# Nearest upsampling by two: the first store copied by VectorE alone and issued by ScalarE

## The chip, the core and the metric

The kernel runs on one core of a Trainium2 chip. The metric is device time in microseconds: the median of 3 runs is 196.97 us (196.87 to 197.55). Of the core's engines the kernel uses VectorE (DVE in the profile) and ScalarE (ACT) to copy, and SyncE (SP) and ScalarE to issue transfers between the chip's main memory (DRAM) and its on-chip memory, which has 128 partitions. The transfers of both issuers run on the core's 16 DMA engines. What SyncE issues stands in one queue (q1 in the profile), what ScalarE issues in another (q10). GpSimd (POOL) and TensorE (PE) do nothing in the kernel but take part in its start and its close.

## The reference

The input is float32 of shape 16 x 64 x 64 x 64 (16.78 MB), the output 16 x 64 x 128 x 128 (67.11 MB). Every input element is written to a block of two by two output elements:

```
for i in range(new_h):
    for j in range(new_w):
        src_i = i // scale_factor
        src_j = j // scale_factor
        result[:, :, i, j] = x[:, :, src_i, src_j].copy()
```

Nothing is computed. One input row of 64 elements becomes two equal output rows of 128, that is 256 elements.

## The kernel before

The 65536 input rows (batch, channel and height taken together) are spread over the 128 partitions, 512 rows each, and every partition's rows are contiguous in main memory, in the input and in the output. So each partition's work is: bring in 512 rows of 64 elements, expand each to 256 elements, write them out.

One tile `mem` holds everything (lines 186 to 188). Its back part `xt` is the input, 512 x 64 elements; its front part of `WF` = 20224 elements is free at first. The expanded rows of a step go to a piece of `mem`, called `u`, and are stored from there.

Three loads are issued by SyncE at the very start (lines 192 to 195, moved ahead of the start barrier by `begin_before_barrier`): rows 0 to 31, rows 32 to 287, rows 288 to 511, being 1, 8 and 7 MB (in the profile's KB: 1024, 8192, 7168). All stand in SyncE's queue, in this order.

Then nine steps, called tiles 0 to 8 here, with 54, 38, 54, 61, 54, 63, 63, 63 and 62 rows (line 181). Each step makes two copies and one store (lines 212 to 216). VectorE expands the first `kv` rows (line 213), ScalarE the others (line 214), both through an access pattern that reads each element twice along the row and each row twice. In tiles 1 to 8 `kv` is five eighths of the rows, cut to an even number: 22, 32, 38, 32, 38, 38, 38, 38. In tile 0 it is all rows but one: 53 on VectorE, 1 on ScalarE. Tile 0 needs the first two loads, since its rows go up to 53.

Store n is issued once both copies of tile n are done. Stores 3 and 5 are issued by ScalarE, the other seven by SyncE. An issuing engine works off its instructions in the order in which the program lists them, and waits at each for what it needs; on ScalarE that means the order copy 0, copy 1, copy 2, copy 3, store 3, copy 4 and so on.

Where the pieces lie sets the order around the change (lines 206 to 208). Tiles 0, 2, 4, 6, 8 lie at the front of `mem`, from element 0 on, so tile 2 may be written only when store 0 has landed, tile 4 when store 2 has landed, and so on. Tiles 1, 3, 5, 7 end where the input rows of their step begin, so they write over input rows that earlier steps have expanded: tile 1's copies wait for VectorE's copy of tile 0, and tile 3's wait for store 1. There are thus two buffers in turn, and a store's landing is what lets the step after next begin. The tile framework puts in these waits by itself.

`close_early` arranges the end of the program: the final wait is on the last SyncE store, the others are waited for by GpSimd earlier.

Of the kernel before, what the change touches and what calls it, by code (L numbers as in the profile page):

```python
# [153 lines left out]
@with_exitstack  # L154
def kernel(
    ctx: ExitStack,
    tc: tile.TileContext,
    x: bass.AP,
    scale_factor: int,
    out: bass.AP,  # L160
):
    nc = tc.nc
    nc.at_finalize(begin_before_barrier)
    nc.at_finalize(close_early)
    P = nc.NUM_PARTITIONS
    s = int(scale_factor)
    B, C, H, W = x.shape
    R = B * C * H // P
    fdt = x.dtype

    xp = x.rearrange("b c h w -> (b c h) w").rearrange("(p r) w -> p r w", p=P)
    op = out.rearrange("b c (h hd) w -> (b c h) (hd w)", hd=s).rearrange(
        "(p r) w -> p r w", p=P
    )

    rows = [54, 38, 54, 61, 54, 63, 63, 63, 62]
    GROW = s * s
    FREE = 79
    WF = FREE * GROW * W
    assert sum(rows) == R
    mem_pool = ctx.enter_context(tc.tile_pool(name="mem", bufs=1))
    mem = mem_pool.tile([P, WF + R * W], fdt, name="mem")
    xt = mem[:, WF:].rearrange("p (r w) -> p r w", r=R)

    HEAD = 32
    cuts = [0, HEAD, R // 2 + HEAD, R]
    for lo, hi in zip(cuts, cuts[1:]):
        nc.sync.dma_start(out=xt[:, lo:hi], in_=xp[:, lo:hi])  # L195

    def expanded(r0, r1):
        return (
            xt[:, r0:r1].unsqueeze(2).unsqueeze(4).to_broadcast([P, r1 - r0, s, W, s])
        )  # L200

    r0 = 0
    before = (0, 0)
    for n, k in enumerate(rows):
        size = k * GROW * W
        at = 0 if n % 2 == 0 else WF + r0 * W - size
        assert at >= before[1] or at + size <= before[0]
        before = (at, at + size)
        u = mem[:, at : at + size].rearrange(
            "p (k a w b) -> p k a w b", k=k, a=s, w=W  # L210
        )
        kv = k - 1 if n == 0 else k * 5 // 8 & ~1
        nc.vector.tensor_copy(out=u[:, :kv], in_=expanded(r0, r0 + kv))  # L213
        nc.scalar.copy(out=u[:, kv:], in_=expanded(r0 + kv, r0 + k))  # L214
        issuer = nc.scalar if n in (3, 5) else nc.sync
        issuer.dma_start(out=op[:, r0 : r0 + k, :], in_=u)  # L216
        r0 += k

# [34 lines left out]
```

## Time and profile before

| quantity | value |
|---|---|
| median of 3 runs | 196.97 us (196.87 to 197.55) |
| profiled execution, own time | 197.08 us |
| its span | 195.7 us |
| VectorE busy | 52.3 us in 9 instructions |
| ScalarE busy | 42.1 us in 10 instructions |
| moved by DMA | 83.89 MB, mean 429 GB/s |
| VectorE, 53 rows of tile 0 (L213) | 14.29 us |
| ScalarE, 1 row of tile 0 (L214) | 0.40 us |
| issue of store 0 by SyncE | at 38.48 us, landed 57.44 |
| issue of store 1 by SyncE | at 42.11 us, landed 68.95 |

The times in the profile count from the span's start. "SPq" and "ACTq" are the issuing sequencers of SyncE and ScalarE. In a group of instructions the columns are the line, the engine, the operation, output and input tile, the shapes (partitions x elements), the count, then the busy time in us and the mean in ns of one, then the idle time of the engine just before them and what ended it. The chain that ended last has the start, the duration and the work of each piece. A DMA's duration in the chain runs from its issue to its landing, so it holds the time in which it stood in its queue behind others. Beside these views the trace records each packet of each DMA (queue, start, duration, size); a packet here is one partition's share of a transfer.

### The profile page before, as it was taken

The page shows a single profiled execution, that of the slowest core. Times are in us where ns is not written, and L with a number is a line of the kernel's source. Part 1 is how long each engine was busy: PE and PEld are TensorE (multiplying, and loading weights), DVE is VectorE, ACT ScalarE, POOL GpSimd, SP SyncE. Part 2 cuts the span into 40 slices and gives each one's busy share as a digit, 9 for nine tenths or more (in the row PEclk, how much of TensorE's full clock was granted, in tenths as well). Part 3 has the DMA queues.
Part 4 walks back from the last instruction along what each step waited for, and adds up shares of the span by engine and source line. Part 5 has one row for each costly group of instructions (what it writes and reads, how often), then busy time and mean ns, then how long its engine had stood idle before and what let it go on. Part 6 is the DMA issues. An engine that isn't in the chain of part 4 may idle for free.

```text
span 195.7 us, 102 instructions
## 1 busy us (share of the span) xinstructions
DVE 52.3 (27%) x9; ACT 42.1 (21%) x10; POOL 0.2 (0%) x4
## 2 busy tenths in 40 slices
DVE  0000099940026081000627200055540063000000
ACT  2000000150029700000694000059700073000000
POOL 0000000000000000000000000000000000000000
DMA  9999989889898989989999899999999999999994
GB/s 429 429 429 429 402 375 562 375 362 542 362 435 382 540 384 441 490 385 406 408 476 475 362 482 488 416 422 422 422 422 422 422 422 422 435 499 493 428 441 208
DMA packets 1728, 83.89 MB, mean 429 GB/s; under 512 B 192, under 2 KB 192, under 8 KB 192
## 3 DMA queue, kind: packets, MB, share of 16 engines
q1 hardware_dynamic: 1440, 67.63, 80.1%
q10 hardware_dynamic: 288, 16.25, 19.2%
HBM read 16.78 MB, written 67.11 MB: 429 GB/s over the span
## 4 chain that ended last, share of the span: by engine, by line
DMA 65%; ACT 11%; DVE 7%; SPq 0%; issue 0%; DVEq 0%; ACTq 0%
DMA out_dram<-mem 53%; DMA mem<-in_x_dram 12%; ACT mem L214 11%; DVE mem L213 7%; SPq L195 0%; DVEq L213 0%; ACTq L214 0%; SPq L216 0%
## 5 line engine op out<-in xcount | busy, mean ns | idle before, releaser
L213 DVE COPY mem<-mem 128x9728 f32<-128x9728 f32 (+3 forms) x9 | 52.3, 5818 | 111.0 <-DMA out_dram<-mem 86.9
L214 ACT COPY mem<-mem 128x6400 f32<-128x6400 f32 (+5 forms) x9 | 40.8, 4530 | 119.6 <-DMA out_dram<-mem 84.4
L214 ACT ACT_TABLE_LOAD x1 | 1.3, 1283 | 1.7 <-PEq L234 1.7
L234 POOL MEMSET const-bfloat16-1.0<- 128x1 bf16 x1 | 0.1, 101 | 0.0
L234 POOL MEMSET const-uint8-127<- 128x1 uint8 x1 | 0.1, 101 | 0.0
L234 POOL MEMSET const-float32-0.0<- 128x1 f32 x1 | 0.1, 98 | 0.2 <-issue 0.2
L234 POOL MEMSET const-float32-1.0<- 128x1 f32 x1 | 0.1, 98 | 0.0
## 6 DMA issues: line engine op xcount, KB each, us to landing
out_dram<-mem SPq DMA_DIRECT2D x3, 6912.0 KB, 30.1
out_dram<-mem SPq DMA_DIRECT2D x2, 8064.0 KB, 27.8
out_dram<-mem ACTq DMA_DIRECT2D x1, 8064.0 KB, 29.9
out_dram<-mem SPq DMA_DIRECT2D x1, 7936.0 KB, 32.3
out_dram<-mem ACTq DMA_DIRECT2D x1, 7808.0 KB, 29.3
mem<-in_x_dram SPq DMA_DIRECT2D x1, 7168.0 KB, 40.2
out_dram<-mem SPq DMA_DIRECT2D x1, 4864.0 KB, 26.8
mem<-in_x_dram SPq DMA_DIRECT2D x1, 1024.0 KB, 4.7
```

The costliest lines, as they stand in the source:

```text
L213: nc.vector.tensor_copy(out=u[:, :kv], in_=expanded(r0, r0 + kv))
L214: nc.scalar.copy(out=u[:, kv:], in_=expanded(r0 + kv, r0 + k))
L234: nc = _bacc.Bacc("TRN2", target_bir_lowering=False, num_devices=1)
```

## The change

In tile 0 VectorE now expands all 54 rows, ScalarE none, and store 0 is issued by ScalarE in place of SyncE. On ScalarE the issue stands where its copy of tile 0 stood, ahead of its copy of tile 1. Tiles 1 to 8 are as they were, and so are the loads.

```
-        kv = k - 1 if n == 0 else k * 5 // 8 & ~1
+        kv = k if n == 0 else k * 5 // 8 & ~1
         nc.vector.tensor_copy(out=u[:, :kv], in_=expanded(r0, r0 + kv))
-        nc.scalar.copy(out=u[:, kv:], in_=expanded(r0 + kv, r0 + k))
-        issuer = nc.scalar if n in (3, 5) else nc.sync
+        if kv < k:
+            nc.scalar.copy(out=u[:, kv:], in_=expanded(r0 + kv, r0 + k))
+        issuer = nc.scalar if n in (0, 3, 5) else nc.sync
         issuer.dma_start(out=op[:, r0 : r0 + k, :], in_=u)
```

## The prediction

> **What bounds the kernel now.** I read the page first, from the utilisation strip down to the DMA queues, to see whether any resource is full.
>
> ```profile
> span 195.7 us, 102 instructions
> ...
> DVE 52.3 (27%) x9; ACT 42.1 (21%) x10; POOL 0.2 (0%) x4
> ...
> DMA  9999989889898989989999899999999999999994
> ...
> q1 hardware_dynamic: 1440, 67.63, 80.1%
> q10 hardware_dynamic: 288, 16.25, 19.2%
> HBM read 16.78 MB, written 67.11 MB: 429 GB/s over the span
> ```
>
> The engines are idle most of the time; the two DMA queues (q1 is issued by SyncE, q10 by ScalarE) together take 99.3% of the 16 DMA engines. The packet records agree: each engine carries 8 of the 128 partitions of a transfer as 8 packets one behind the other, the first packet starts at 1.01 us, the last ends at 195.37, and in between no engine has a gap. A packet moves 27.1 bytes per ns, load or store (65536 B in 2.42 us, 55296 B in 2.04, 38912 B in 1.44), so the bytes alone need this time. An edit that only moves work about can win next to nothing here; what it can do is open a gap, and a gap in a full stream comes back at the end, whole. So the question is whether the DMA engines still always have a packet.
>
> Next the chain that ended last, in order of time, and the groups of instructions by shape.
>
> ```profile
> 24.11 14.30 DVE mem L213
> ...
> 38.48 18.96 DMA out_dram<-mem
> ...
> 57.47 4.89 ACT mem L214
> ...
> 62.38 32.09 DMA out_dram<-mem
> ```
> ```profile
> L213 DVE COPY mem<-mem 128x9728 f32<-128x9728 f32 x5 | 26.1, 5227 | 50.5 <-DMA out_dram<-mem 50.5
> ...
> L213 DVE COPY mem<-mem 128x13568 f32<-128x13568 f32 x1 | 14.3, 14286 | 24.1 <-DMA mem<-in_x_dram 24.1
> ...
> L213 DVE COPY mem<-mem 128x8192 f32<-128x8192 f32 x2 | 8.9, 4426 | 36.4 <-DMA out_dram<-mem 36.4
> ...
> L214 ACT COPY mem<-mem 128x4096 f32<-128x4096 f32 x1 | 3.6, 3607 | 14.0 <-DVE mem L213 14.0
> L213 DVE COPY mem<-mem 128x5632 f32<-128x5632 f32 x1 | 3.1, 3083 | 0.0
> ```
>
> Tile 0 is copied from 24.11 to 38.41. Its store is issued at 38.48 and lands at 57.44. Only then is its buffer free for tile 2, whose copies take until 62.36, and store 2 is issued at 62.38. What covers that stretch is store 1: in the SyncE queue it stands behind store 0, and its packets run until 68.57 on the last engine. So store 2 comes about 6.2 us before the stream would run dry. This slack is what I follow.
>
> Last, the timeline of two stores, because it shows what two queues do to each other.
>
> ```profile
> 62.38 0.33 SPq L216 DMA_DIRECT2D out_dram<-mem  x1
> ...
> 74.39 0.37 ACTq L216 DMA_DIRECT2D out_dram<-mem  x1
> ```
>
> Store 2 (8 packets of 2.04 us per engine, 16.3 us) starts at 67.93 to 68.57 and is alone until store 3, from the ScalarE queue, joins. From then on the packet records of each engine alternate one by one: store 3 (2.31 us), store 2 (2.04), store 3, and so on. So store 2 lands at 94.46, not near 85. Three rules can be read there. The queues share by whole packets, in turn. The small packet that signals the end takes a turn of its own, so on 14 engines, where store 2's data ended near 88.9, the signal went out near 91.2; on the other two at 94.05 to 94.08, 0.4 before the landing. And the ScalarE queue gets its first packet late: issue 74.39, first packet 78.73 (+4.34) on the engine nearest to it, while one whose packet ended at 78.64 (+4.25) let the other queue go once more; store 5 shows +4.27 taken, +4.06 not. So the threshold is about 4.26 us after the issue, at the next packet boundary.
>
> **The change part by part.** The sum is made against the profiled execution, which took 197.08 (span 195.7 and 1.4 around it), 0.11 above the median 196.97; differences are then put on the median.
>
> *The copy.* Out go VectorE's 53 rows (14.29 us) and ScalarE's single row (0.40 us, already hidden beside them); in come 54 rows on VectorE, 13824 elements. The shapes of 22, 32 and 38 rows take 3.08, 4.43 and 5.23 us, a line of 0.523 ns per element plus 0.14 us; 53 rows stand off it at 1.05 ns. On the line 54 rows take 7.37 us, at the rate of 53 rows 14.56. I take 7.37: the row count is even as in the three fast shapes. The trace alone can't tell oddness from mere length. The Trainium skill, VectorE: DVE Perf Modes, section "Mode 2×_2P — use both read ports for one tensor", says that the two-port mode wants an outermost dimension that is even; by it the price is the 7.37 too. The copy ends at 24.11 + 7.37 = 31.48, 6.9 us earlier. In itself this is worth nothing: the DMA engines are at the third load until 40.13 to 40.76.
>
> *The issue moves to ScalarE.* By the row 74.30 (VectorE's end, 69.07 + 5.23) to 74.39 it comes 0.09 after the copy, at 31.57. Behind it on ScalarE is the 16-row copy of tile 1 (3.61 us), which waits for VectorE's copy anyway, as the 14.0 us wait above shows; it starts 0.37 later and ends near 35.6, and SyncE, rid of its first wait, issues store 1 there instead of at 42.11. If the activation table load (1.28 us, at 1.73 now) slips behind the new wait, store 1 comes at 36.9. Both are hidden: the third load holds the SyncE queue until past 42.
>
> *The third load, the stores 0 and 1.* The threshold 31.57 + 4.26 = 35.83 falls onto the packet boundaries of the third load, 35.82 to 36.34, so I work out both cases. On the engine with the latest skew store 0 begins at 36.34. It has two load packets (2.12) and the load's signal as partners, and from 48.7 on store 1's packets (1.44): store 0's eighth packet ends at 62.65, then one of store 1 to 64.09, then the signal, landed near 64.5. On an engine whose boundary was at 35.82 store 0 begins at 37.94 and has one more packet of store 1 between: signal at 65.02, landed at 65.4. One such engine decides, as the landing needs all 16. So store 0 lands at 64.5 to 65.4 in place of 57.44, though it began 4 us earlier: it now runs beside store 1, in the old order ahead of it. The load lands near 46.7, in place of 41.06; its rows (from 288 on) are first needed at tile 5, near 94.6: hidden.
>
> *Tile 2.* Its two copies and the issue need 4.94 us (57.44 to 62.38): issue at 69.4 to 70.3. Meanwhile the same bytes have gone through: store 1's last packet ends at 68.5 as before. Then both queues are empty. First data after an issue into free engines: at least 1.01 us (the first load, issued at 0.00), at most 1.65 (store 0, 38.48 to 40.13, the boundary it may have waited for). Store 2 thus begins at 70.4 to 72.0: a gap of 1.9 to 3.5 us on the engine that ends last, where there was none. Middle 2.7.
>
> *After it.* Store 3 hangs on store 1's landing (68.95) and tile 3's copies behind those of tile 2: VectorE is done at 74.7 to 75.6, where it was 74.30, so store 3 joins store 2 after four or five packets of it, now five or six. With four, store 2 lands near 99.2 and store 4 is issued at 104.2; the queues run dry at 105.8, and 1.01 to 1.65 fit in just so. With five there are some 2 us to spare. Tiles 5 to 8 keep their distances, all moved by the gap. Nothing later wins it back, since no engine had a gap to give. A loss beside it: on the engines that saw their neighbours start storing, the last load packet took up to 2.28 instead of 2.12; two packets like it are 0.3 us at most; a gain from loads mixed with stores I put at 0 to 0.3 as well, there being no row for it.
>
> Sum: 0 (copy) + 0 (issue) + 2.7 (gap) + 0 (after) = +2.7 us, 199.7.
>
> **The rivals.** *(a) No gap.* It is on the other side: no slower, 196.97. Mechanism: store 0 gets more than every second turn, or begins so early that it lands in time. The point: landing by 68.5 − 4.94 − 1.01 to 1.65 = 61.9 to 62.6. For it: only two packets' worth is missing. Against: strict turns from 78.73 on. Real gain would need loads and stores to run faster mixed; the slower load packets at 38 to 40 speak against that.
>
> *(b) Store 0 begins one packet earlier*, at 33.7 to 34.2. It then lands at 62.6 to 63.2, store 2 is issued near 68.1, and the gap is 0.5 to 1.2: 197.5 to 198.1. For it: the 4.3 us were seen on engines in the middle of stores, not loads. The Trainium skill, DMA: Bandwidth & Descriptors, section "Latency and other measured facts", gives about 0.6 us to the first byte for this kind of issue; ready at 32.2, the next boundary would be this one. The trace's two rows, 4.27 and 4.34, disagree, so I give it little.
>
> *(c) The queues share by bytes, finer than the records show.* Then store 0 from about 32.6 runs at half rate beside the third load (7.5 us of its own left, so 15) and store 1 (8.8 of 11.5, so 17.6): landed near 65.6, gap 3.1 to 3.7 with the issue at 70.6: 200.1 to 200.7.
>
> *(d) The change does not do what it says*: the copy stays at 1.05 ns and takes 14.56. Store 0 is issued at 38.76 and finds the SyncE queue almost empty, store 1 follows at 42.8 and is taken up at the boundary near 48.5 after four packets, then four pairs of 3.48 and one more packet: landed near 64.6, gap 2 to 3, and up to 0.3 at 40.1: 199 to 200.3. The same time by another way: the move of the queue alone would do the harm.
>
> **How the numbers follow.** Forecast, a gap of 1.9 to 3.5: 0.68, time 198.9 to 200.5, likeliest 199.7. Rivals: (a) 0.07, (b) 0.08, (c) 0.09, (d) 0.04; 0.04 for more than one gap, above 201. A measurement of this kernel can tell about 0.5%, 1.0 us, so slower means above 197.95. Faster gets 0.02 out of (a); within, the rest of (a) and most of (b), 0.10; slower 0.88. The range 198.0 to 201.0 takes in the forecast with its 0.3 for mixed traffic, (c) and (d), and leaves out (a), most of (b) and the second gap.
>
> **What would show it.** In the profile after: one copy of 128x13824 near 7.4 us and none of 256 elements; an issue of store 0 from ACTq near 31.6 with a landing some 33 us later, longer than the 19.0 now; the third load landing near 46.7; the wait for a store's landing before tile 2 ending at 64.5 to 65.4; and a hole in the DMA strip near 69 to 72 us, with all 16 engines free. The prediction is wrong if store 0 lands before 62.6, or if a hole there is made good later.

## The result, and the profile after

The changed kernel takes 201.63 us (201.56 to 201.72, 4 runs) beside 197.01 for the kernel before in the same comparison: ratio 1.023, 95% interval 1.021 to 1.0249, so 4.6 us slower. The forecast was 199.7 with a range of 198.0 to 201.0: the sign is right, the size is not, and the time lies above the range.

The page of the changed kernel, the same lines as before:

```profile
span 200.2 us, 100 instructions
...
DVE 45.3 (23%) x9; ACT 41.7 (21%) x9; POOL 0.2 (0%) x4
...
DMA  9999999898999888998999898899999999999994
...
q1 hardware_dynamic: 1296, 60.56, 71.0%
q10 hardware_dynamic: 432, 23.33, 27.2%
HBM read 16.78 MB, written 67.11 MB: 419 GB/s over the span
```

The copying engines have less to do than before, and the same bytes take longer: 419 GB/s in place of 429. The two queues together now fill 98.2% of the 16 DMA engines, and even that overstates it: a packet counts as busy for as long as it is open, also when it is held up.

The group of the new copy, and the start of the chain that ended last:

```profile
L213 DVE COPY mem<-mem 128x13824 f32<-128x13824 f32 x1 | 7.4, 7361 | 24.2 <-DMA mem<-in_x_dram 24.2
```
```profile
24.17 7.37 DVE mem L213
31.54 0.02 issue
31.56 35.17 DMA out_dram<-mem
66.73 0.02 issue
66.75 4.89 ACT mem L215
71.64 0.02 issue
71.66 26.96 DMA out_dram<-mem
```

The copy takes 7.36 us for 54 rows, where 53 took 14.29, and store 0 is issued at 31.56, 6.9 us sooner. It lands at 66.73, 9.3 us later than before, 35.17 us after its issue. So tile 2 can begin only at 66.75, and store 2 is issued at 71.66 in place of 62.38. One stretch of time in the view by windows (the columns are the stretch, its length, the busy time of VectorE, ScalarE and GpSimd with the number of instructions, the TensorE clock, the DMA share and GB/s; a packet is counted where it starts), first of the changed kernel, then of the one before:

```profile
70.60:72.50 1.90, 1.90 (x2) 1.87 (x2) 0.00 (x0) 1.00 0.00 0
```
```profile
70.60:72.50 1.90, 1.90 (x1) 0.00 (x0) 0.00 (x0) 1.00 0.94 407
```

In the changed kernel no packet starts between 70.60 and 72.50, and the last one before had ended at 70.56, so nothing at all moves; the kernel before moved 407 GB/s there. This is the forecast gap, where it was forecast.

It is less than half of the loss. On the DMA engine that ends last, store 1's last packet ends at 70.56 in place of 68.57, though the bytes up to there are the same: 1.99 us. Then the gap until store 2's first packet at 72.51: 1.95 us. From there to the end of the last packet it takes 127.33 us (199.84), before 126.80 (195.37 less 68.57): 0.53. (On the mean of the 16 engines this stretch is 0.38 us longer; the rest is where the last engine stands among them.) The three make the 4.47 us between the two ends. The gap was in the forecast; the other two terms, 2.5 us, were not. The packet records say where the first of them arose. Each transfer is 8 packets per engine; the table has the mean duration over the 16 engines of the third load's sixth, seventh and eighth packet and of store 0's first two, in us:

| kernel | load, 6th | 7th | 8th | store 0, 1st | 2nd |
|---|---|---|---|---|---|
| before | 2.12 | 2.13 | 2.22 | 2.04 | 2.05 |
| changed | 3.48 | 2.27 | 2.23 | 2.26 | 2.29 |

The sixth load packet, in flight from about 34.0 to 37.5, is longer by 1.36 us on the mean and long on all 16 engines (3.23 to 3.72); the other four together are longer by 0.6. That is the 1.99. It happens exactly where the first packet of store 0 comes next.

### The profile page after: what moved, and what is told of

It reads as the page before. It is cut to its first block, busy times and chain, and to the rows that moved or that the text cites. A ratio compares the mean times of both kernels' runs of the same rounds, so it can differ in the third digit from the quotient of the medians.

```text
span 200.2 us, 100 instructions
## 1 busy us (share of the span) xinstructions
DVE 45.3 (23%) x9; ACT 41.7 (21%) x9; POOL 0.2 (0%) x4
## 4 chain that ended last, share of the span: by engine, by line
DMA 69%; ACT 10%; DVE 4%; SPq 0%; issue 0%; DVEq 0%; ACTq 0%
DMA out_dram<-mem 58%; DMA mem<-in_x_dram 12%; ACT mem L215 10%; DVE mem L213 4%; SPq L195 0%; DVEq L213 0%; ACTq L215 0%
## 5 line engine op out<-in xcount | busy, mean ns | idle before, releaser
L213 DVE COPY mem<-mem 128x9728 f32<-128x9728 f32 (+3 forms) x9 | 45.3, 5048 | 122.4 <-DMA out_dram<-mem 98.3
L215 ACT COPY mem<-mem 128x6400 f32<-128x6400 f32 (+4 forms) x8 | 40.4, 5046 | 94.0 <-DMA out_dram<-mem 93.9
## 6 DMA issues: line engine op xcount, KB each, us to landing
mem<-in_x_dram SPq DMA_DIRECT2D x1, 7168.0 KB, 48.5
```

## The experiments

The theory after the result: the loss is made of the queues, namely of loads and stores that run mixed (2.0), of a gap by turn-taking (1.95) and of slower packets after it (0.5). The rivals were the faster copy, the activation table load (which had slipped to 32.03, behind ScalarE's new wait), and the first use of ScalarE's queue. Times of the kernel before in the runs below are 197.33 to 197.37.

**The copy alone.** The diff against the changed kernel:

```
-        issuer = nc.scalar if n in (0, 3, 5) else nc.sync
+        issuer = nc.scalar if n in (3, 5) else nc.sync
```

> The copy alone: 54 rows on VectorE in one instruction, store 0 still issued by SyncE behind the third load. Theory (the loss is made of queues only): the copy takes 7.37 us as in the changed kernel, ends near 31.5, store 0 starts at 40.1 to 40.8 as before and lands near 57.4; time 197.0, ratio 1.000 within 0.003. Rival (the faster copy itself disturbs the running load, since the packets of the third load that were in flight from 33.7 to 37.6 in the changed kernel took 3.2 to 3.7 us where 2.12 is usual): those packets are long here too, the stream ends 1.0 to 1.4 us later, about 198.2.

Measured 198.31, ratio 1.0044 (1.0029 to 1.0059): 0.95 us slower. The theory's 197.0 was wrong, and the number is that of the rival. But its reason can't hold: the packets from 33.7 on take 2.12 here; the long one is the third load's last, 3.25 us on the mean, open from about 38.5 to 41.7, when both engines had finished their copies at 35.4. The DMA issues (columns: issuer, KB, us from issue to landing) show the load landing 41.4 us after its issue, where the kernel before has 40.2:

```profile
mem<-in_x_dram SPq DMA_DIRECT2D x1, 7168.0 KB, 41.4
```

So it is again the load packet just ahead of the first store packet that is held up, now in one and the same queue. What the two kernels have in common, and the kernel before does not, is a store that lies ready well before that packet begins: issued at 31.75 here, at 38.48 before. From this came the next two runs.

**The copy alone, with the store held back.** VectorE copies rows of tile 0 a second time, 30 of them in one run, 4 in the other (against the run above):

```
         nc.vector.tensor_copy(out=u[:, :kv], in_=expanded(r0, r0 + kv))
+        if n == 0:
+            nc.vector.tensor_copy(out=u[:, :30], in_=expanded(r0, r0 + 30))
```

> The copy alone (store 0 on SyncE), with store 0 held back: VectorE copies 30 rows of tile 0 a second time, so that the store is issued near 38.6 as before and no longer at 31.75. Theory (a store whose packets lie ready while a load's packet is in flight stretches that packet by some 1.2 us; ready means issued about 2.2 us before that packet begins): the third load's last packet, from 38.4 on, goes back from 3.0 to 3.5 us to 2.1 to 2.4 us, store 0 starts near 40.4, and the time is that of the kernel before within 0.2%. Rival (the fast copy of 54 rows disturbs the load, or the chip run has it so): the packet stays at 3.3 us and the time 0.95 us above before.

> As the run with the late issue, but with only 4 rows copied a second time: store 0 is issued by SyncE near 35.3, in the middle between 31.75 and 38.5. Theory (what counts is whether the store lies ready when the last load packet begins at 38.4, not how long): the packet takes 3.0 to 3.5 us, the time is 0.95 us above before, as with 31.75. Rival (the longer it lies ready, the more it disturbs): about half of that, 0.4 to 0.6.

With 30 rows: 197.46, ratio 1.001 (1.0001 to 1.0019); the load's last packet takes 2.12. With 4 rows: 198.42, ratio 1.0055 (1.004 to 1.007); it takes 3.25, as without the delay. The chains, first with 30 rows, then with 4:

```profile
24.24 10.36 DVE mem L213 x2
34.60 4.08 DVE mem L215
38.68 0.02 issue
38.70 18.86 DMA out_dram<-mem
```
```profile
24.64 10.36 DVE mem L213 x2
35.01 0.61 DVE mem L215
35.62 0.02 issue
35.64 23.38 DMA out_dram<-mem
```

The same fast copy of 54 rows stands in all three runs. Issued at 38.70 the store costs 0.1 us, at 35.64 and at 31.75 about the same 1 us (1.1 and 0.95). So the copy is cleared, and between these two it makes no difference how long the store lies there: what matters is whether it is ready when the last load packet starts, near 38.5. How far ahead it must be issued is bounded by the changed kernel: the fifth load packet, begun 0.05 to 0.6 us after the issue at 31.56, kept its 2.12 us; the sixth, begun 2.2 to 2.7 us after it, did not. The slow odd-row copy of the kernel before brings the issue to 38.48, just late enough: its last load packet took 2.22 us on the mean, 2.45 at most.

**The queue alone.** The kernel before, with store 0 issued by ScalarE:

```
-        issuer = nc.scalar if n in (3, 5) else nc.sync
+        issuer = nc.scalar if n in (0, 3, 5) else nc.sync
```

> The queue alone: tile 0 copied as before (53 rows on VectorE at 14.29 us, 1 row on ScalarE), store 0 issued by ScalarE at about 38.6, when the third load is nearly through. Theory (three terms of the changed kernel's 4.5 us: 2.0 from packets slowed while loads and stores run mixed, 1.95 from the gap ahead of store 2, 0.5 from slower packets after it): the first term all but vanishes, because no load is left; the turn-taking with store 1 stays, store 0 lands at 64 to 65.5, a gap of 1.5 to 2.8; time 199.0 to 200.2. Rival (the 2.0 come with the first use of ScalarE's queue, whatever runs beside it): 201 to 202. Rival (a gap needs the early start): 197.0.

Measured 201.78, ratio 1.0221 (1.0206 to 1.0236), as slow as the whole change, though no load packet is long here (2.12 to the last). This is above what the theory gave, and agrees in number with the rival; the parts tell why. Store 0's first packets take 2.83 where 2.04 is usual, 0.8 us. The gap is longer, 3.3 us on the last engine (69.39 to 72.71): when the last of store 0's signals goes out (66.51), store 1 has two packets left on the mean of the engines; in the changed kernel (66.25) it has three. From the gap to the end it takes 127.33 us, as in the changed kernel. The chain:

```profile
38.71 28.22 DMA out_dram<-mem
66.92 0.02 issue
66.95 4.90 ACT mem L214
71.84 0.02 issue
71.86 26.97 DMA out_dram<-mem
```

**Store 1 in ScalarE's queue too, first try.** Against the changed kernel:

```
-        issuer = nc.scalar if n in (0, 3, 5) else nc.sync
+        issuer = nc.scalar if n in (0, 1, 3, 5) else nc.sync
```

> The changed kernel with store 1 issued by ScalarE too, so that it stands behind store 0 in the same queue and does not take turns with it; the third load still runs beside store 0. Theory: store 0 meets only two or three load packets, lands near 59.5, store 2 is issued near 64.5 and store 1 still runs until 70.5, so there is no gap; the slowing beside the loads, 2.0 us, stays: 199.0. If the gap costs more than its 1.95 by the state it leaves (0.5 slower packets after it), that goes as well. Rival (the queues' turns are not the cause of the late landing): store 0 lands at 66 and the time stays at 201.6.

Measured 201.28, ratio 1.0193 (1.0178 to 1.0209). The edit did more than was meant: in the program as built, store 1's issue stands behind ScalarE's copy for tile 2, which waits for store 0's landing, so store 1 was issued at 59.84 and a gap opened ahead of it:

```profile
59.78 4.89 ACT L215 COPY mem<-mem 128x5632 f32<-128x5632 f32 x1 [22.84 <-DMA out_dram<-mem]
59.84 0.34 ACTq L217 DMA_DIRECT2D out_dram<-mem  x1
```

As a test of the gap it decides nothing, except that store 0 without store 1 as a partner lands at 59.76 and not at 66. It shows something else: on engines that had run dry, store 1 began at 60.68 to 60.83 out of ScalarE's queue, 0.84 us after its issue at the earliest, as soon as store 2 does out of SyncE's in the changed kernel (71.66 to 72.51, 0.85).

**The same with the order kept.** ScalarE's copy of tile 2 is put behind store 1's issue:

```
+            if n == 2:
+                with tc.issue_after(store.ins):
+                    nc.scalar.copy(out=u[:, kv:], in_=expanded(r0 + kv, r0 + k))
...
+        issuer = nc.scalar if n in (0, 1, 3, 5) else nc.sync
+        store = issuer.dma_start(out=op[:, r0 : r0 + k, :], in_=u)
```

> The changed kernel with store 1 issued by ScalarE as well, now with the issue kept ahead of tile 2's copy on ScalarE (near 37), so that store 1 stands right behind store 0 in one queue. Theory (gap by turn-taking): store 0 meets three load packets at most, lands near 59.5, store 2 is issued near 64.5, store 1's packets run until 70.5: no gap. The slowing beside the load, about 2.0 us, remains: 2.0 us above before, ratio 1.010; the 2.5 us of gap and slower packets behind it are gone. Rival (turns don't matter, a store in ScalarE's queue beside a load lands late by itself): store 0 lands at 64 or later and the ratio is 1.02.

Measured 199.22, ratio 1.0106 (1.0081 to 1.0132). The chain:

```profile
31.69 27.88 DMA out_dram<-mem
59.57 0.02 issue
59.59 4.89 ACT mem L217
64.48 0.02 issue
64.50 27.40 DMA out_dram<-mem
```

Store 0 is issued as early as in the changed kernel and meets the same load (sixth packet 3.34, first two of store 0 2.19 and 2.21), but it takes no turns with store 1: it lands at 59.57, 7.2 us sooner, and the DMA engines never run dry; the window that was empty in the changed kernel is full:

```profile
70.60:72.50 1.90, 0.00 (x0) 0.00 (x0) 0.00 (x0) 1.00 1.41 612
```

The packets after it have their old length, 2.380 for 63 rows and 2.041 for 54. Of 4.6 us only the 1.9 beside the load are left. So the gap and the slower packets after it, 2.5 us in the changed kernel's trace, go with the turn-taking.

**The gap alone.** The kernel before, with VectorE's part of tile 2 copied twice, and 8 rows three times more:

```
         nc.vector.tensor_copy(out=u[:, :kv], in_=expanded(r0, r0 + kv))
+        if n == 2:
+            nc.vector.tensor_copy(out=u[:, :kv], in_=expanded(r0, r0 + kv))
+            nc.vector.tensor_copy(out=u[:, :8], in_=expanded(r0, r0 + 8))
...
```

> The kernel before with a gap made by hand: VectorE copies its 32 rows of tile 2 a second time and 8 of them three times more, about 8.1 us, so that store 2 is issued near 70.1 in place of 62.4, while store 1's packets end at 68.6. First data 0.85 us after the issue, as in the changed kernel, gives a gap of 2.3 us on the engine that ends last. Theory (a gap comes back whole, and the packets after it are 0.2 to 0.3% longer because all 16 engines then run in step, 0.5 us): 2.8 us above before, ratio 1.014. Rival (the 0.5 us came with the load and store mixing, not with the gap): 2.3 us, packets after the gap at 2.041 and 2.380. Rival (a gap is made good later): no change.

Measured 200.27, ratio 1.0149 (1.0134 to 1.0164): 2.9 us. Store 2 is issued at 70.39, its first packet on the last engine starts at 71.22, and store 1's last ended at 68.69: a gap of 2.53. The windows:

```profile
69.00:71.00 2.00, 1.97 (x3) 0.61 (x1) 0.00 (x0) 1.00 0.00 0
71.00:73.00 2.00, 2.00 (x1) 2.00 (x1) 0.00 (x0) 1.00 1.04 442
```

Nothing is made good later; on the contrary, from there to the end of the last packet it takes 127.33 us, as in the changed kernel and 0.53 more than before. The packets are longer as in the changed kernel: 2.386 against 2.380 us for 63 rows, 2.050 against 2.041 for 54. No load runs here beside a store any more than before, so the third term belongs to the gap. What the records show beside it: before the gap the 16 engines start their packets spread over 0.6 us, after it within 0.15. That the longer packets come from the engines running in step fits all five kernels here in which they ran dry, but was not tried by itself.

**The table load.** One small copy on ScalarE ahead of store 0's issue, so that the activation table is loaded at the start again:

```
+        if n == 0:
+            nc.scalar.copy(out=mem[:, size : size + W], in_=xt[:, k - 1])
         issuer = nc.scalar if n in (0, 3, 5) else nc.sync
```

> The changed kernel, with one more small copy on ScalarE (one input row of 64 elements into a free piece that nobody reads) ahead of store 0's issue, so that the activation table load goes back to 1.7 us and the 16-row copy and store 1's issue come 1.28 us sooner. Theory (loads and stores mixed slow each other): nothing changes, 201.6, the third load's packet at 34 still takes over 3.2 us. Rival (the table load at 32.0, or store 1's issue at 36.95, blocks the DMA engines): that packet takes 2.1 us, and the time falls by 1.1 to 1.4 us to 200.3.

Measured 201.77, ratio 1.0218 (1.0201 to 1.0235), and the sixth load packet takes 3.25 with the table load at 1.74. So the table load has no part in it. Nor has store 1's issue: it moved only from 36.95 to 35.98 here, but in the first try above it came at 59.84, and the packet took 3.32 there. Two of the six runs took 202.7 to 202.8, the profiled one among them: in it one engine sent store 0's signal at 67.53, a turn behind the other fifteen (64.89 to 66.16), and the landing waits for all 16.

**Late, in ScalarE's queue, without turns; and with that queue used before.** The first is the queue alone, with store 1 by ScalarE and the order kept as above; the second adds a load of the last row by ScalarE:

```
-    cuts = [0, HEAD, R // 2 + HEAD, R]
+    cuts = [0, HEAD, R // 2 + HEAD, R - 1]
...
+    nc.scalar.dma_start(out=xt[:, R - 1 :], in_=xp[:, R - 1 :])
```

> The queue alone, late, and without turns: tile 0 copied as before (store 0 issued by ScalarE near 38.7), and store 1 issued by ScalarE too, right behind its copy. In the run with the queue alone the first packets of store 0 took 2.83 us where 2.04 is usual, then came the turns with store 1 and the gap. Theory (the loss of that run is the gap by turns, and 0.8 us of a late first packet): no gap here, the first packets still 2.8 us, 0.8 us above before, ratio 1.004. Rival (a late store in ScalarE's queue costs more than its first packet): ratio over 1.010.

> As the run late and without turns, with one change: the last input row (row 511, 32 KB in all) is loaded by ScalarE at the start, so that ScalarE's queue has been used before store 0. Theory A (the 0.8 us of store 0's first packet is the price of the first use of ScalarE's queue): the first packets take 2.04 to 2.1 us, and the time is that of before. Theory B (it is the delay with which ScalarE's queue takes up any store, 2.2 us and more after the issue, while SyncE's takes 1.65 at most): first packets 2.8 us again, 0.8 us above before.

Measured 197.93, ratio 1.0029 (1.0016 to 1.0041), and 198.16, ratio 1.004 (1.0025 to 1.0055). Store 0's first packets take 2.54 and 2.79 us on the mean. Without turns the queue alone costs 0.6 us in place of 4.4; and the 0.6 to 0.8 do not come from a first use, since in the second run the queue had been used. SyncE's queue has no such price at the same moment: in the run with the late issue, issued at 38.70, its first packets start at 40.35 to 40.80 and are 2.05 long.

Theory B, a late take-up of ScalarE's queue, isn't shown, and the records speak against it. The first packets are open from 40.37 to 40.82 on, as soon as the load has ended and 1.6 to 2.0 us after the issue. In the first run seven of the 16 take 2.09 us, nine 2.74 to 3.15, and an engine whose packet began later than its neighbour's is often done sooner. And into idle engines ScalarE's queue delivered 0.84 us after the issue, as the first try showed. Why these packets are long stays open.

## Why the prediction was wrong in size

*What bounds the kernel.* Right. The stream was full, a gap came back whole, and nothing made it good; the run with the gap alone shows this by itself.

*The copy.* 7.37 forecast, 7.36 measured. The Trainium skill, VectorE: DVE Perf Modes, section "Mode 2×_2P — use both read ports for one tensor", names an even outermost dimension as the condition (or an odd one that is equal in source and destination), and this run agrees: one row more than 53, and half the time. "In itself this is worth nothing" failed: with the store left on SyncE it costs 0.95 us, because it makes the store ready too early. I looked only at whether the DMA engines were busy, not at what an early store does to the load in front of it.

*The issue.* Right: 31.56 for the forecast 31.57; the table load slipped behind the wait, store 1 was issued at 36.95 for 36.9, and both stayed hidden. The third load landed at 49.4 (48.5 us after its issue) for the forecast 46.7, hidden too.

*Threshold and turns.* The turns are right. The threshold is not borne out, though one of the two cases worked out from it came. The load packets that were in flight began at 33.74 to 34.27, and on every engine store 0's came next, the early one of the two cases. But these packets were stretched, so their ends fell at 37.24 to 37.71, 5.7 us and more after the issue, so no engine tried a threshold of 4.26. Nor is the late start a mark of ScalarE's queue: in the run with the order kept, SyncE's store 2, issued at 64.50 among store 1's packets of 1.44 us in ScalarE's queue, began at +3.72 on the first engine. What fits these issues is another reading: a queue that joins busy engines comes next behind a packet that began some 2.1 to 2.3 us or more after the issue (from 2.18 us in the changed kernel, 2.29 in that run, 2.13 in the run with the early table load; for store 3 in the kernel before 2.30 was followed, 2.21 not). From the first turn on, load and store alternate as forecast. The Trainium skill, DMA: Bandwidth & Descriptors, section "Queues, rings and completion order", has engines take turns between queues packet by packet; the records agree, with one partition's whole share of 38 to 63 KB as the unit.

*"Two packets like it are 0.3 us at most."* This is the step that failed. I took the last load packet of the kernel before, 2.12 to 2.28, as the price of a load beside stores. The reading was short (two of its 16 packets took 2.40 and 2.45), but that would have made it 0.7 at most. The main thing is that the store was issued at 38.48, too late to lie ready when the packet began. The price of a ready one is 1.1 to 1.4 us for the first packet, and 0.6 for the turns after: 2.0 in place of 0.3. No row of the trace showed it, and the bound should then have been left open upwards.

*The landing and the gap.* Store 0 landed at 66.73 for 64.5 to 65.4: the early case plus those 2.0, and 0.2 more. The gap was 1.95, in the forecast 1.9 to 3.5, at its lower end: all engines took the early case, store 1's end moved by the same 2.0 as the landing, and the 0.2 more was made up by the first data, which came 0.85 us after the issue, below my bound of 1.01. That it meets the bound so closely is luck; that it is there is not.

*"After it: 0."* Short by 0.5: the packets behind a gap are 0.2 to 0.5% longer.

*The rivals.* (a), (b) and (c) did not come. Of (d) the slow copy did not come, but its remark that the move of the queue alone would do the harm is shown, though with 201.8 and not 199 to 200.3, since the gap is 3.3 there and the long first packet costs 0.8.

The sum as it should read: 2.0 beside the load, 1.95 gap, 0.5 after it, 4.5 in all.

## What to carry to other kernels

Here, with the DMA engines full from end to end, a second queue gave no time; it changed who lands when. Where a buffer hangs on a landing, ask with what the transfer will take turns: here store 0 began earlier, took turns with the younger store 1, and landed 9.3 us later. Before a store is made ready sooner, look at what is in flight: ready behind a load it held that load up, and a slower copy that issues it just in time was the better one. A price that the trace of before doesn't show stays open upwards in a range.

## What the runs showed of the hardware that was not expected

A load packet in flight took 3.25 to 3.48 us in place of 2.12 when a store, issued some 2.1 us or more before it began, came next behind it, in the same queue (3.25) or in the other (3.25 to 3.48). When the store was issued only after the packet had begun, it took 2.11 to 2.12 in five runs and 2.22 in the kernel before. Why is open: the packet records show only that it is open longer.

After a gap in which all 16 engines ran dry, their packets were longer to the end: 2.386 against 2.380 us, and 2.050 against 2.041.

A store issued into ScalarE's queue shortly before the loads ended had first packets of 2.54 to 2.83 us on the mean, one into SyncE's queue at the same moment 2.05. Why is open.

ScalarE's queue is not slow of itself: into idle engines its first packet came 0.84 us after the issue, SyncE's 0.85. Into engines busy with the other queue the first packet came late from either: 4.34 us after the issue for ScalarE's in the kernel before, 3.72 for SyncE's in the run with the order kept.
